# One weight split and one head's loads issued earlier in a fused attention and recurrence layer

## The chip, the cores and the metric

The kernel runs on one core of one Trainium2 chip. The metric is device time in microseconds (us); lower is better. The engines named below are TensorE (PE, matrix products; PEld is its weight load), VectorE (DVE), ScalarE (ACT), GpSimd (POOL) and SyncE (SP), which issues most of the transfers. Each engine works through its own list of instructions in order; between engines an instruction waits for the events it depends on.

## The reference

One layer of a hybrid encoder on 1024 tokens of width 1024, all in float32. Cut to what matters:

```python
h = layer_norm(x, emb_ln_g, emb_ln_b)
q, k, v, z_a, u, z_b, g_a, g_b = split(h @ w_in)
attn = neighbourhood_attention(q, k, v, rpb)     # 8 heads of 64, a window of 8 x 16 on a 16 x 64 grid
y_a = attn * silu(z_a)
u = centred_depthwise_conv(u, conv_w, conv_b)
h2 = rg_lru(u, ..., forward) + rg_lru(u, ..., reverse)
y_b = h2 * silu(z_b)
m = sigmoid(g_a + b_merge[0]) * (y_a @ w_ba) + sigmoid(g_b + b_merge[1]) * (y_b @ w_bb)
out = layer_norm(ALPHA * h + m @ w_out, ln_g, ln_b)
```

## The kernel before

Every large product is made of three: both operands are split into a high part in the matmul's own format and the low rest, and the kernel adds high x high, high x low and low x high (`mm3`, line 127). A weight tile therefore needs two instructions before it can be used: a cast that makes the high part, and a subtraction (`lo_of`, lines 124 and 125) that makes the low part.

The stages follow one another: the first layer norm and the v and q projections; sixteen pairs of projection columns with seven products each (`product`, slots 0 to 111), with the recurrence woven in; a short `ending`; attention; the merge of the two branches with their gates; the output product with the last layer norm. All engines' lists are in the order in which the Python code issues instructions; only buffers and waits are filled in behind.

**Between the projections and attention.** At slot `HEAD_AT` = 109 memory comes free, and `load_k(0)` (line 862) brings the keys of head 0 (1 MB with both copies; queries and bias of head 0 are loaded three slots earlier). In slots 112 to 114 `ending` (line 958) runs the first product of the recurrence branch's projection, in two column halves on two banks; it loads their gate tiles (`g_load(1, 0, k)`, line 939, 256 KB each), which VectorE multiplies in `b_gate` (line 954). In its third step it loads the next weight tile, two further gate tiles and, through `load_head(1)` (line 868), what head 1 needs: queries `qs` (line 858, 512 KB), bias (line 859, 448 KB) and keys `ks` (line 864, 1024 KB). Meanwhile the last gate results of the projections are still being stored (`gb_d`, line 652). All these transfers are issued by SyncE. The first load of values, `load_v(0)` (line 1026), follows.

**Attention.** Work goes in units of one block of 128 queries. A unit of head h holds `biased` (VectorE adds the bias to a score, line 1046), `turned` (TensorE transposes probabilities, line 1058), `values` (line 1082), `exped` (ScalarE, line 1051) and `score` for head h+1 (TensorE, line 1036), and some matmuls of the recurrence branch's projection as filling. Scores go into two banks in turn. Head 1's first score comes in unit 0, right behind the first transposes of head 0.

**The merge.** Eight weight tiles of the attention branch (`wb`, tag with two buffers) are used one after another; tile j serves two slots, one for each half n of the columns, with twelve matmuls each. `b_split(0, j, A)` (line 835) casts the high part on ScalarE (line 840) and makes the low part on GpSimd. `merge(j, n)` (line 1237) applies the gate and adds the other branch on VectorE (lines 956 and 1239), then casts the high part of the result on ScalarE (line 1241); `merge_lo` makes its low part. The output weights `wo` are split in the same loop (line 1280 on ScalarE, then GpSimd). The first two slots are irregular: their last three matmuls (k = 3 of tile 0) are held back until attention's last head is done, so tile 0 is read for the last time at the end of slot 2:

```python
run(b_group(0, j, n, ya, o, range(3 if slot < 2 else 4)))
if 0 < slot < 3:
    run(b_group(0, 0, slot - 1, ya, sums_m[slot - 1], range(3, 4)))
    merge(0, slot - 1, sums_m[slot - 1])
if n == 0 and j > 0:
    b_split(0, j + 1, A)
```

Tile (0,2), the third, is split in slot 2 and used from slot 4 on.

Of the kernel before, what the change touches and what calls it, by code (L numbers as in the profile page):

```python
# [35 lines left out]
HEAD_AT = 109  # L36
# [31 lines left out]
def encoder_kernel(ctx, tc, x, gb1, gb, w_qk, w_v, w_s, w_ba, w_bb, w_gate, smalls, bias, w_out, out):  # L68
# [3 lines left out]
    def pool(name, side="left", **kw):  # L72
        return tc.alloc_tile_pool(name=name, bufs=1, side=side, reuse_waits="tile", **kw)
# [13 lines left out]
    def bank(name):  # L87
        if turns:
            return banks[0].tile([P, HALF], F32, tag=next(turns[0]), bufs=2, name=name)
        return banks[0].tile([P, HALF], F32, tag="bank", name=name)  # L90
# [23 lines left out]
    def pair(pl, shape, name, **kw):  # L114
        return [pl.tile(shape, F32R, name=f"{name}_{c}", **({**kw, "tag": kw["tag"] + c} if "tag" in kw else kw))
                for c in "hl"]
# [7 lines left out]
    def lo_of(eng, lo, full, hi):  # L124
        eng.tensor_tensor(lo, full, hi.bitcast(F32), ALU.subtract)  # L125
# [10 lines left out]
    def run(gen):  # L136
        for _ in gen:
            pass
# [538 lines left out]
    def at(slot, pos, f):  # L677
        todo.setdefault((slot, pos), []).append(f)
# [151 lines left out]
    def b_load(which, j):  # L830
        if j < NK:
            st = b_w[which, j] = ev.tile([P, 4, P], F32, tag="z", bufs=5, name=f"wb{which}{j}")
            SP.dma_start(st[:], (w_ba, w_bb)[which][j])

    def b_split(which, j, eng=None):
        if j < NK:
            st = b_w[which, j]
            hi, lo = b_w[which, j] = pair(late["wb"], [P, 4, P], f"wb{which}{j}", tag="wb", bufs=2)
            if eng is A:
                A.copy(hi[:], st[:])  # L840
            else:
                G.tensor_copy(hi[:], st[:])  # L842
            lo_of(G, lo[:], st[:], hi[:])
# [10 lines left out]
    def load_q(h):  # L854
        hd = late["hd" if h % 2 else "hd0"]
        q = hd.tile([P, S], F32R, tag="qs", name=f"qs{h}")
        bt = hd.tile([P, BIAS_W], F32, tag="bias", name=f"bias{h}")
        SP.dma_start(q[:].bitcast(F32), q_d[h // 2][HALVES[h % 2][0]].rearrange("p z s -> (p z) s"))
        SP.dma_start(bt[:], bias[h])
        heads[h] = q, bt  # L860

    def load_k(h):
        k = late["hd"].tile([P, 2, S], F32R, tag="ks", bufs=2, name=f"ks{h}")
        SP.dma_start(k[:].rearrange("p z s -> p (z s)").bitcast(F32),
                     k_d[h // 2][HALVES[h % 2][0]].rearrange("p z s -> p (z s)").unsqueeze(1).to_broadcast([DH, 2, 2 * S]))
        heads[h] = heads[h][0], k, heads[h][1]

    def load_head(h):
        if h < H:
            load_q(h)  # L870
            load_k(h)
# [21 lines left out]
        at(slot + 3, 0, lambda t=t: yb_lo(t))  # L893
    at(HEAD_AT, 1, head_pool)
    at(HEAD_AT, 1, lambda: load_k(0))
    at(HEAD_AT - 3, 1, head_start)

    RHS = dict(a11=B11, s2=T2, s3=T3, s1=T1, a12=B21, a22=T4, s4=B22)
# [40 lines left out]
    def g_load(which, j, n, **kw):  # L939
        if j < NK:  # L940
            g = mt[which, j, n] = ev.tile([P, HALF], F32, name=f"g{which}{j}{n}", **(kw or dict(tag="z", bufs=5)))
            SP.dma_start(g[:], (ga_d, gb_d)[which][j][:, n * HALF:(n + 1) * HALF])

    def b_group(which, j, n, y, o, ks=range(4)):

        yield from mm3(o[:], [([t[:, k, :] for t in b_w[which, j]], [t[:, k, halves[n]] for t in y]) for k in ks],
                       quantum=1, first=ks[0] == 0, last=ks[-1] == 3)

    def b_gate(which, j, n, o):
        sl = slice(n * HALF, (n + 1) * HALF)  # L950
        g = mt.pop((which, j, n))
        if which == 1:
            m1 = late["m", j, n] = late["mp"].tile([P, HALF], F32, tag=f"m{j}{n}", name=f"m1{j}{n}")
            V.scalar_tensor_tensor(m1[:], g[:], 1.0, o[:], ALU.add, ALU.mult)
        else:
            V.scalar_tensor_tensor(o[:], g[:], 1.0, o[:], ALU.add, ALU.mult)

    def ending(k):

        if k == 0:  # L960
            for pl in (hts.pop(), hts.pop(), wsp, hb):
                pl.release()
            late["mp"] = pool("mp")
        if k == 2:
            b_load(1, 2)
            for n in range(2):
                g_load(1, 1, n)
            load_head(1)
        if k < 2:
            g_load(1, 0, k)  # L970
            late["o", k] = bank(f"mb10{k}")
            run(b_group(1, 0, k, late["yb"], late["o", k]))
        if 0 < k < 3:
            b_gate(1, 0, k - 1, late["o", k - 1])
# [3 lines left out]
    for slot in range(7 * N_PAIR + 4):  # L978
        p, k = divmod(slot, 7)
        if k == 0 and p < N_PAIR:  # L980
            takers[p], ub[p] = takes[p](), {}
        done = (p, k - 1) if k else (p - 1, 6)
        prep = (p + 1, OPS[k - 1]) if k else (p if p else N_PAIR, OPS[6])
        rest = evacuate(*done) if slot <= 7 * N_PAIR else []
        s_hi(*prep)
        for f in todo.pop((slot, 0), ()):
            f()
        for f in squashes:
            f()
        squashes = rest[:1]  # L990
        stores[slot + 2] = rest[1:]
        if p < N_PAIR:
            product(p, k)
        for o in lows:
            s_lo(*o)
        lows = [prep]
        for f in stores.pop(slot, ()):
            f()
        if k < 4:
            s_sum(p + 1, ("s1", "s2", "s3", "s4")[k])  # L1000
        elif k == 4:
            s_load(p + 2, "a11", "a21", "a12", "a22")
        for f in todo.pop((slot, 1), ()):
            f()
        if p == N_PAIR:
            ending(k)
# [156 lines left out]
    for unit in range(-NT, H * NT + PV_LAG):  # L1163
# [50 lines left out]
        if unit == H * NT:  # L1214
# [7 lines left out]
            def w_load(k):  # L1222
                if k < NK:
                    wos[k] = wop.tile([P, D], F32, tag="wos", bufs=3, name=f"wos{k}")
                    SP.dma_start(wos[k][:], w_out[k * P:(k + 1) * P, :])
# [9 lines left out]
    sums_m, mh, ml = {}, {}, {}  # L1235

    def merge(j, n, o):
        b_gate(0, j, n, o)
        V.tensor_tensor(o[:], o[:], late["m", j, n][:], ALU.add)
        mh[j, n] = late["mp"].tile([P, HALF], F32R, tag=f"m{j}{n}", name=f"mh{j}{n}")  # L1240
        A.copy(mh[j, n][:], o[:])

    def merge_lo(j, n, o):
        lo_of(V, ml[j, n][:], o[:], mh[j, n][:])
# [8 lines left out]
    for slot in range(2 * NK + 2):  # L1253
        j, n = divmod(slot, 2)
        if 2 < slot <= 2 * NK:
            merge(*divmod(slot - 1, 2), sums_m[slot - 1])
        if slot == 2:
            at0.release()
            mlp = pool("mlp")
            ml.update({(j, n): mlp.tile([P, HALF], F32R, name=f"ml{j}{n}") for j in range(NK) for n in range(2)})  # L1260
            wo += [pair(mlp, [P, D], f"wo{k}") for k in range(NK - 2, NK)]
            merge_lo(0, 0, sums_m.pop(0))
        for q in (1,) if slot == 3 else (slot - 2,) if slot > 3 else ():
            merge_lo(*divmod(q, 2), sums_m.pop(q))
        if j < NK:
            if n == 0:
                b_load(0, j + 2)
            g_load(0, j + 1, n, **(dict(tag=f"u{slot % 4}", bufs=1) if slot % 4 else dict(tag="z", bufs=5)))
            o = sums_m[slot] = bank(f"mb{j}{n}")

            run(b_group(0, j, n, ya, o, range(3 if slot < 2 else 4)))
            if 0 < slot < 3:
                run(b_group(0, 0, slot - 1, ya, sums_m[slot - 1], range(3, 4)))
                merge(0, slot - 1, sums_m[slot - 1])
            if n == 0 and j > 0:
                b_split(0, j + 1, A)

        if slot % 2:
            if j < NK:
                A.copy(wo[j][0][:], wos[j][:])  # L1280
            if j > 0:
                w_load(j + 2)
        elif slot > 0:
            lo_of(G, wo[j - 1][1][:], wos.pop(j - 1)[:], wo[j - 1][0][:])
        if slot == 9:
            zp = pool("zp")
            gb2 = zp.tile([P, 2, D], F32, name="gb2")
            zs = {}

            def load_z(i):  # L1290
                if i < NT:
                    zs[i] = zp.tile([P, D], F32, tag="z", bufs=4, name=f"z{i}")
                    SP.dma_start(zs[i][:], h_d[i])

        elif slot in (10, 12, 14):
            load_z(slot // 2 - 5)
        elif slot in (11, 13):
            SP.dma_start(gb2[:, :, halves[slot // 13]], gb[slot // 13])
# [146 lines left out]
```

## Time and profile before

| | |
|---|---|
| time, median of 3 runs | 683.49 us (683.47 to 684.93) |
| time of the profiled execution | 684.63 us |
| its span, first to last instruction | 682.8 us |
| its mean granted TensorE clock | 0.997 |
| matmul instructions | 3177 |
| moved by transfers | 113.40 MB, mean 166 GB/s |

A row of the profile's timeline has the start in us from the span's start, the length, the engine, the line of the kernel, the operation, output<-input and the number of instructions; in brackets stands the idle time before it and what ended that. SPq is SyncE's queue of issues: such a row is the issue of a transfer, not its duration. A row of waits has the waiting instruction, what it waited for, the total in us, how often, and the longest.

### The profile page before, as it was taken

What the parts mean: (1) busy time and instruction counts of PE and PEld (TensorE: products, weight loads), DVE (VectorE), ACT (ScalarE), POOL (GpSimd) and SP (SyncE); (2) the same over time, 40 slices, a digit from 0 to 9 for tenths busy, and PEclk for the clock granted to TensorE, in tenths of its full rate; (3) what the DMA queues carried; (4) which work ended last, traced back from release to release, by engine and by line L of the source; (5) the groups of instructions that cost most, each with busy time, mean ns of one, the idle gap of its engine ahead of it and who ended that gap; (6) DMA issues with size and microseconds to landing.
All of it is one profiled execution on the core that took longest, in us unless ns stands there. A gap on an engine that the chain in (4) does not pass through costs nothing.

```text
span 682.8 us, 9299 instructions
## 1 busy us (share of the span) xinstructions
PE 665.8 (98%) x3177; PEld 554.4 (81%) x3177; DVE 494.7 (72%) x821; ACT 363.9 (53%) x612; POOL 353.8 (52%) x258
## 2 busy tenths in 40 slices
PE   7999999999999999999999999999999999999995
PEld 6787888888888888888788888788888878888884
DVE  7866766796899599879977785378787777533434
ACT  4544524247686677768576634467777554310110
POOL 5697461444576577567647544115355446435442
PEclk9999999999999999999999999999999999999998
DMA  8654165223324233431453557898794457512211
GB/s 327 227 187 154 63 231 171 78 92 124 124 92 145 71 108 123 170 124 48 170 199 112 182 176 253 305 353 308 250 327 144 176 197 271 189 62 93 92 62 61
DMA packets 48703, 113.40 MB, mean 166 GB/s; under 512 B 5057, under 2 KB 9745, under 8 KB 47121
## 3 DMA queue, kind: packets, MB, share of 16 engines
q1 hardware_dynamic: 48624, 112.81, 47.4%
q8 instruction: 25, 0.41, 0.2%
q14 instruction: 22, 0.17, 0.1%
q10 hardware_dynamic: 32, 0.01, 0.0%
HBM read 77.11 MB, written 35.68 MB: 165 GB/s over the span
## 4 chain that ended last, share of the span: by engine, by line
PE 80%; DVE 8%; DMA 4%; POOL 3%; issue 2%; ACT 1%; SPq 1%; DVEq 0%; POOLq 0%; ACTq 0%
PE a L131 29%; PE o L131 13%; PE s L131 11%; PE mb L131 10%; PE q L131 5%; PE acc L1082 3%; PE pt L1058 3%; PE s L1036 3%; POOL x L243 2%; PE v L308 2%; PE g L734 2%; DMA wvsl<-in_w_v_dram 1%; DMA ks<-k_d 1%; DMA wb<-in_w_ba_dram 1%; DVE ws_l L125 1%
## 5 line engine op out<-in xcount | busy, mean ns | idle before, releaser
L131 PE MATMUL o<-wo_h,ml 128*128 128x512 f32 (+1 forms) x136 | 51.2, 377 | 0.0
L131 PE MATMUL o<-wo_l,mh 128*128 128x512 f32 (+1 forms) x136 | 51.2, 376 | 0.0
L131 PE MATMUL o<-wo_h,mh 128*128 128x512 f32 (+1 forms) x136 | 51.2, 376 | 0.0
L1046 DVE CUSTOM_DVE_ANT_0 sc<-s,bias 128x384 f32<-128x384 f32 (+1 forms) x64 | 33.5, 523 | 22.9 <-PE s L1036 14.0
L131 PE MATMUL a<-ht_h,ws_h 128*128 128x512 f32 x128 | 49.9, 390 | 0.0
L131 PE MATMUL a<-ht_h,ws_l 128*128 128x512 f32 x128 | 49.8, 389 | 0.0
L131 PE MATMUL a<-ht_l,ws_h 128*128 128x512 f32 x128 | 49.8, 389 | 0.0
L131 PE MATMUL a<-b_h,wa_h 128*128 128x512 f32 x128 | 49.8, 389 | 0.0
L131 PE MATMUL a<-b_h,wa_l 128*128 128x512 f32 x128 | 49.8, 389 | 0.0
L131 PE MATMUL a<-b_l,wa_h 128*128 128x512 f32 x128 | 49.8, 389 | 0.0
L1335 DVE SCALAR_TENSOR_TENSOR z<-z,o 128x512 f32<-128x512 f32 (+1 forms) x17 | 11.2, 656 | 51.0 <-PE o L131 51.0
L1066 ACT CAST pt_h<-pt 128x384 fp32r<-128x384 f32 x64 | 29.0, 453 | 26.4 <-PE pt L1058 18.3
L1345 POOL TENSOR_TENSOR z<-z,gb 128x1024 f32<-128x1024 f32 x7 | 16.8, 2395 | 48.5 <-ACT z L1344 48.5
L1051 ACT ACTIVATE p<-sc,summ 128x384 f32<-128x384 f32 (+1 forms) x64 | 37.9, 592 | 5.2 <-DVE summ L1046 5.0
L1314 ACT ACTIVATE sd<-mv,eps_z 128x1 f32<-128x1 f32 x8 | 2.4, 294 | 67.1 <-DVE mv L1340 67.1
L308 PE MATMUL v<-wv,b_h 128*128 128x512 f32 x128 | 32.8, 399 | 2.7 <-ACT b_h L263 1.6
L125 DVE TENSOR_TENSOR pt_l<-pt,pt_h 128x384 fp32r<-128x384 f32 x64 | 33.2, 519 | 2.1 <-ACT pt_h L1066 1.6
L1036 PE MATMUL s<-ks,qs 128*128 128x384 f32 (+1 forms) x128 | 31.3, 326 | 1.1 <-DMA ks<-k_d 1.1
L308 PEld LDWEIGHTS v<-wv,b_h 128*128 128x128 f32 x128 | 23.6, 188 | 9.3 <-ACT b_h L263 2.3
L842 POOL CAST wb_h<-wb 128x512 fp32r<-128x512 f32 x9 | 7.0, 777 | 46.1 <-PE s L1036 18.3
L125 POOL TENSOR_TENSOR wb_l<-wb,wb_h 128x512 fp32r<-128x512 f32 x16 | 22.0, 1374 | 16.1 <-ACT wb_h L840 15.4
L1058 PEld LDWEIGHTS pt<-ident,p 128*128 128x128 f32 x176 | 23.1, 140 | 8.5
(438 smaller groups left out, 2199.8 us busy)
## 6 DMA issues: line engine op xcount, KB each, us to landing
ks<-k_d SPq DMA_DIRECT2D x8, 1024.0 KB, 8.0
h_d<-x SPq DMA_DIRECT2D x8, 512.0 KB, 4.4
v_d<-vs SPq DMA_DIRECT2D x8, 512.0 KB, 3.7
q_d<-q SPq DMA_DIRECT2D x8, 512.0 KB, 3.0
ga_d<-ga SPq DMA_DIRECT2D x16, 256.0 KB, 2.0
gb_d<-gb SPq DMA_DIRECT2D x16, 256.0 KB, 2.0
k_d<-k SPq DMA_DIRECT2D x8, 512.0 KB, 4.0
qs<-q_d SPq DMA_DIRECT2D x8, 512.0 KB, 3.9
```

The source lines that it names most:

```text
L125: eng.tensor_tensor(lo, full, hi.bitcast(F32), ALU.subtract)
L131: PE.matmul(o, a, b, start=first and i == 0, stop=last and i == len(prods) - 1, skip_group_check=not (first and last))
L243: G.tensor_tensor(z[:, halves[c]], z[:, halves[c]], gb_t[w][c][:], op)
L308: PE.matmul(vos[i][:], a, wv[kind == "w"][k][:], start=vn[i] == 0, stop=vn[i] == 23)
L734: PE.matmul(o[:, n, :], w[:, 2 * d + b, :], us[b][:, n * HALF:(n + 1) * HALF], start=z == 0, stop=z == 1)
L1036: PE.matmul(o[:, :P * len(near(t))], q[:, t * P:(t + 1) * P], k[:, z, keys], start=z == 0, stop=z == 1)
L1046: V.tensor_tensor_reduce(s[:, :w], o[:, :w], heads[h][2][:, b0:b0 + w], -1.0, 3.0e38, ALU.add, ALU.min, accum_out=sums[h][0][:, t:t + 1])
L1051: A.activation(probs[h % 2][t][:], scs.pop((h, t))[:, :w], AF.Exp, bias=sums[h][0][:, t:t + 1], scale=-1.0, accum_out=sums[h][1][:, t:t + 1])
L1058: PE.transpose(tp[:, n * P:(n + 1) * P], probs[h % 2][t][:, z * P:(z + 1) * P], ident[:])
L1066: A.copy(pt[0][:, span(b)], tps[h, b][:, :P * len(near(b))])
L1082: PE.matmul(acc[g][:, d:d + w], vvs[h // 2][:, b, h % 2, :], pt[:, a:a + w], start=b in (1, 6) and z == 0, stop=z == 1 and b == (4, 7)[g])
L1345: G.tensor_tensor(z[:], z[:], gb2[:, 0, :], ALU.mult)
```

## The change

Two edits. `load_head(1)` moves from the third step of `ending` to slot `HEAD_AT`, right behind `load_k(0)`. And in the merge loop `b_split` stands between the held-back matmuls and their `merge`; among the slots to which both apply (1 and 2) only slot 2 has n = 0 and j > 0, so it is the split of tile (0,2) that moves, ahead of `merge(0, 1)`. All other instructions stay, in number and order.

```diff
     at(HEAD_AT, 1, head_pool)
     at(HEAD_AT, 1, lambda: load_k(0))
+    at(HEAD_AT, 1, lambda: load_head(1))
     at(HEAD_AT - 3, 1, head_start)
...
             b_load(1, 2)
             for n in range(2):
                 g_load(1, 1, n)
-            load_head(1)
         if k < 2:
...
             if 0 < slot < 3:
                 run(b_group(0, 0, slot - 1, ya, sums_m[slot - 1], range(3, 4)))
-                merge(0, slot - 1, sums_m[slot - 1])
             if n == 0 and j > 0:
                 b_split(0, j + 1, A)
+            if 0 < slot < 3:
+                merge(0, slot - 1, sums_m[slot - 1])
```

## The prediction, made before the changed kernel ran

> **What bounds the kernel now.** I read the busy shares first, then TensorE's waits, then the chain that ended last, and last the instructions around the two places that the change touches. The page's first part:
>
> ```profile
> PE 665.8 (98%) x3177; PEld 554.4 (81%) x3177; DVE 494.7 (72%) x821; ACT 363.9 (53%) x612; POOL 353.8 (52%) x258
> ```
>
> TensorE is busy for 98% of the span. Only its idle time, or another order of its work, can be won, and this change leaves TensorE's order alone. The view of waits for TensorE has these rows from 443 us to the end, and no others there:
>
> ```profile
> PE s L1036 <- DMA ks<-k_d: 1.1, 1, 1.1
> PE mb L131 <- POOL wb_l L125: 0.9, 1, 0.9
> PE mb L131 <- ACT wb_h L840: 0.5, 1, 0.5
> ```
>
> One wait is for the keys of a head; the other two are one stall, for the two halves of a weight tile. The chain that ended last runs through both:
>
> ```profile
> 434.73 8.79 DMA ks<-k_d
> ...
> 542.23 6.96 DMA wb<-in_w_ba_dram
> ...
> 553.49 1.29 POOL wb_l L125
> 554.82 32.71 PE mb L131 x143
> 587.53 87.36 PE o L131 x408
> ```
>
> Columns: start, length, what. After 554.82 TensorE works without a gap until the last products, so a microsecond taken out before it should reach the end.
>
> **First part: the second head's loads.** The keys `ks1` are issued at 434.73 and land at 443.52. TensorE around that moment:
>
> ```profile
> 442.10 0.49 PE L1058 MATMUL pt<-ident,p 128*128 128x128 f32 x3
> 443.65 0.47 PE L1036 MATMUL s<-ks,qs 128*128 128x256 f32 x2 [1.07 <-DMA ks<-k_d]
> ...
> 445.68 0.49 PE L1058 MATMUL pt<-ident,p 128*128 128x128 f32 x3
> 445.93 0.59 PE L1036 MATMUL s<-ks,qs 128*128 128x384 f32 x2
> ```
>
> Unhindered, a score starts 0.25 us after its three transposes (445.68 to 445.93). The stalled one started 1.55 us after, so the stall cost 1.30 us, a little over the 1.07 shown as idle. The three loads (queries, bias, keys) now stand right behind the first head's keys in SyncE's queue:
>
> ```profile
> 422.37 0.55 SPq L864 DMA_DIRECT2D ks<-k_d  x1
> 426.66 0.32 SPq L652 DMA_DIRECT2D gb_d<-gb  x1
> 427.07 0.38 SPq L942 DMA_DIRECT2D g<-gb_d  x1
> 429.72 0.38 SPq L942 DMA_DIRECT2D g<-gb_d  x1
> ...
> 433.79 0.42 SPq L858 DMA_DIRECT2D qs<-q_d  x1
> ...
> 436.70 0.54 SPq L1029 DMA_DIRECT2D vv<-v_d  x1
> ```
>
> The queue rests from 422.92 until the gate store at 426.66; three issues of some 0.5 us fit into that pause, so `ks1` is issued by about 424.5. What did 1 MB of keys take?
>
> ```profile
> DMA to landing us min/median/max: 4.7/8.0/9.2
> ```
>
> Even the longest, 9.2, lands at 433.7, against a need at 442.35. So the 1.30 us go, and head 0's own keys, 4.7 us alone, are wanted only for the first score, which VectorE reads at 436.58 (row below).
>
> What is late next? The loads are 512, 448 and 1024 KB; from 427 on they share the engines with two gate stores and the two gate loads of `ending` (256 KB each): 3,008 KB, 3.08 MB, up to the second gate load. VectorE needs those two loads here:
>
> ```profile
> 433.26 0.69 DVE L954 SCALAR_TENSOR_TENSOR m<-g,mb 128x512 f32<-128x512 f32 x1 [4.75 <-PE mb L131]
> 435.98 0.69 DVE L954 SCALAR_TENSOR_TENSOR m<-g,mb 128x512 f32<-128x512 f32 x1 [2.03 <-PE mb L131]
> 436.58 0.42 DVE L1046 CUSTOM_DVE_ANT_0 sc<-s,bias 128x256 f32<-128x256 f32 x1
> ```
>
> Queued behind the second `L954` on VectorE is the first biased score, and TensorE has two score banks, so it can run only two scores ahead of VectorE. A gate load later than 435.98 costs TensorE at most that lateness. How fast does the queue empty? Two rows of the view by stretches (the last two figures: share of the DMA engines, GB/s):
>
> ```profile
> 434.00:436.00 2.00, 2.00 (x11) 1.69 (x10) 0.02 (x1) 0.00 (x0) 0.00 (x0) 1.00 0.88 223
> 436.70:443.60 6.90, 5.88 (x31) 4.96 (x29) 4.64 (x17) 5.61 (x17) 1.30 (x1) 1.00 1.02 409
> ```
>
> The second stretch carries the same kinds of load and is full; at 409 GB/s 3.08 MB take 7.5 us. `ks0` landed at 422.37 + 4.7 = 427.07, so the second gate load would be in by 434.6: 1.4 us to spare. At the slowest, 223 GB/s, it would be 13.8 us and 440.9, a loss of 4.9. The first row is two microseconds in which the loads were only being issued, so I take the full stretch, and nothing for this cost; 0 to 4.9 stays for the range. The first `L954` may slip by 2 us without harm, since the gap of 2.03 us in front of the second hides it.
>
> The Trainium skill ("DMA: Bandwidth & Descriptors", section "Queues, rings and completion order") speaks against the move: each DMA engine takes descriptors in ring order, so a load issued behind 2 MB stands behind all of it. The same page puts the memory side at about 358 GB/s, which would make it 8.6 us and 435.7; the 409 in the row is above that. By the page the sum would be the same, with 0.3 us to spare.
>
> SyncE waits in order as well. In the changed kernel's instruction list the second (1,1) gate load waits for the first `L954` (over at 433.95) and, since eight completion counters are used in turn, for `ks1`; the first values load `vv` stands behind it. That puts `vv` at about 434.4 at the latest, against 436.70 before, while its reader comes only 1.3 us earlier. No cost.
>
> **Second part: the weight split.** In the changed list on ScalarE, the cast `wb_h` of tile (0,2) moves up past one cast, `mh` of (0,1); the cast of (1,0) already stood behind it. Nothing is added. ScalarE, GpSimd and TensorE there:
>
> ```profile
> 550.11 1.05 ACT L1280 CAST wo_h<-wos 128x1024 fp32r<-128x1024 f32 x1
> 552.31 0.58 ACT L1241 CAST mh<-mb 128x512 fp32r<-128x512 f32 x1 [1.15 <-DVE mb L1239]
> 552.79 0.62 ACT L840 CAST wb_h<-wb 128x512 fp32r<-128x512 f32 x1
> ...
> 555.56 0.59 ACT L1241 CAST mh<-mb 128x512 fp32r<-128x512 f32 x1 [0.39 <-DVE mb L1239]
> 556.04 0.62 ACT L840 CAST wb_h<-wb 128x512 fp32r<-128x512 f32 x1
> ```
> ```profile
> 553.49 1.28 POOL L125 TENSOR_TENSOR wb_l<-wb,wb_h 128x512 fp32r<-128x512 f32 x1 [7.76 <-ACT wb_h L840]
> 554.72 2.40 POOL L125 TENSOR_TENSOR wo_l<-wos,wo_h 128x1024 fp32r<-128x1024 f32 x1
> 557.08 1.30 POOL L125 TENSOR_TENSOR wb_l<-wb,wb_h 128x512 fp32r<-128x512 f32 x1
> ```
> ```profile
> 549.86 0.39 PE L131 MATMUL mb<-ya_l,wb_h 128*128 128x512 f32 x1
> ...
> 552.58 0.39 PE L131 MATMUL mb<-ya_l,wb_h 128*128 128x512 f32 x1
> 553.46 0.50 PE L131 MATMUL mb<-ya_h,wb_h 128*128 128x512 f32 x1 [0.50 <-ACT wb_h L840]
> 554.82 0.50 PE L131 MATMUL mb<-ya_h,wb_l 128*128 128x512 f32 x1 [0.86 <-POOL wb_l L125]
> 555.16 0.40 PE L131 MATMUL mb<-ya_l,wb_h 128*128 128x512 f32 x1
> ```
>
> The split can start when three things are there: its data (the chain's load, 542.23 + 6.96 = 549.19), its buffer (the last matmul that reads tile (0,0), 549.86 + 0.39 = 550.25) and ScalarE (`wo_h`, 550.11 + 1.05 = 551.16). The last decides: `wb_h` runs from 551.16 to 551.78, 1.6 us earlier. GpSimd, idle by then, follows 0.08 behind as before (553.41 to 553.49), 551.86 to 553.15. TensorE's twelve matmuls from 549.86 to 552.58 are 0.227 apart, so tile (0,2) is first wanted at 552.81, its low half at 553.03 and its high half again at 553.26. With the low half at 553.15 the second matmul starts near 553.2, and the third 0.23 to 0.34 later (0.34 is the spacing behind the old stall), at 553.43 to 553.54. It was at 555.16: a gain of 1.6 to 1.7; I take 1.7. The passed cast waits for VectorE until 552.3 anyway and loses nothing. If the load landed after 551.16 instead, the gain would shrink one for one.
>
> Late next would be tile (0,3). Its `wb_h` stays at 556.04, tied to VectorE through the cast at 555.56, but `wo_l` no longer stands in GpSimd's way (553.15 to 555.55), so `wb_l` runs from 556.74 to 558.04. TensorE wants it 24 matmuls (5.44 us) after 553.2, at 558.64. 0.6 us of slack; not a stall.
>
> **Sum.** 1.3 + 1.7 = 3.0 us. The profiled execution had a span of 682.8 and a time of 684.6 (1.8 outside the span), and would come to 681.6. The three runs shown are 683.47 to 684.93 with the profiled one near the top; from their median, 683.5 - 3.0 = 680.5.
>
> **Rivals.**
>
> *Only the split pays.* The profiled execution is 1.1 us above the median, about the size of the keys' stall. If that stall is small in most runs, or a late gate load gives the 1.3 back, 1.7 remains: 681.8. For it: landings vary widely for one size (4.7 to 9.2). Against it: the chain ties the issue of `ks1` to a store and a blocked queue, which any run has.
>
> *The split only moves the stall.* If tile (0,3) or VectorE's order of merges turns out to be what TensorE then waits for, little of the 1.7 stays: 683.5 - 1.3 = 682.2. Against it is the slack of 0.6, for it that this was computed with GpSimd at its usual 1.3 us.
>
> *Gate loads behind the 2 MB (slower).* Place: the second `L954`. Price: one for one from 435.98. It cancels both gains when the load takes over 9.3 us from its issue at 429.72, and shows as slower from 10.6 us. The gate loads of the whole run:
>
> ```profile
> DMA to landing us min/median/max: 2.5/4.9/8.5
> ```
>
> The median gives 434.6, the maximum 438.2 and a loss of 2.2, still a net gain. Only at the 223 GB/s would it land at 440.9: 683.5 - 3.0 + 4.9 = 685.4.
>
> **How the numbers follow.** Both gains: 0.67 (680.5). Only the split, or a partial loss at the gate loads: 0.17 (681.8). The stall moved: 0.11 (682.2). Slower: 0.05 (685.4). The range 679.6 to 682.4 holds the first three, with 0.9 below the forecast for two stalls that are larger in other runs than in the profiled one. 0.2% is 1.4 us, about what a measurement of this kernel tells from no change, so faster means below 682.1: the first case, nearly all of the second and a little of the third, 0.84; same 0.11; slower 0.05.
>
> **What would show it.** Right: no wait of TensorE for `ks` and the scores of head 1 straight behind the transposes; `ks1` landed before 434; `wb_h` ahead of the `mh` cast near 551 on this clock (some 549.9 with the first gain) and under 0.3 us of wait for `wb_l`. Wrong: a wait of `L954` for a gate load near 436 with TensorE stalled at the third score, a `wb` wait one tile later, or a new wait in the heads between, where the profile of before shows none.

## The result, and the profile after

| | before | changed |
|---|---|---|
| median of the runs | 683.48 us (683.09 to 684.93, 6 runs) | 681.35 us (681.14 to 681.54, 6 runs) |
| profiled execution: time, span | 684.63, 682.8 us | 681.54, 679.8 us |
| granted TensorE clock | 0.997 | 0.997 |

The ratio is 0.9963, with a 95% interval of 0.9950 to 0.9976: the kernel became faster, by 1.6 to 3.4 us. The medians alone differ by 2.1; here and below the ratio is not the quotient of the medians, so the two can differ by some tenths of a us. In the two profiled executions the difference is 3.0 in the span.

The view of waits for TensorE, from 400 us to the end of the changed kernel, has one row left in place of three:

```profile
PE mb L131 <- DVE ya_l L125: 0.2, 1, 0.2
```

The keys and both halves of the weight tile are gone from it. TensorE's timeline of the changed kernel at head 1's first score, with the first matmul of `ending` ahead of it (start, length, engine, line, operation):

```profile
429.89 0.39 PE L131 MATMUL mb<-yb_h,wb_h 128*128 128x512 f32 x1
...
441.65 0.49 PE L1058 MATMUL pt<-ident,p 128*128 128x128 f32 x3
441.89 0.48 PE L1036 MATMUL s<-ks,qs 128*128 128x256 f32 x2
```

The score now starts 0.24 us after its transposes, not 1.55. SyncE's queue in the changed kernel, and the first two gate products on VectorE:

```profile
421.92 0.55 SPq L864 DMA_DIRECT2D ks<-k_d  x1
422.53 0.59 SPq L858 DMA_DIRECT2D qs<-q_d  x1
423.16 0.42 SPq L859 DMA_DIRECT2D bias<-in_bias_dram  x1
423.63 0.54 SPq L864 DMA_DIRECT2D ks<-k_d  x1
...
426.63 0.39 SPq L943 DMA_DIRECT2D g<-gb_d  x1
...
429.23 0.48 SPq L943 DMA_DIRECT2D g<-gb_d  x1
...
435.78 0.42 SPq L1029 DMA_DIRECT2D vv<-v_d  x1
```
```profile
434.33 0.69 DVE L955 SCALAR_TENSOR_TENSOR m<-g,mb 128x512 f32<-128x512 f32 x1 [6.26 <-DMA g<-gb_d]
435.64 0.69 DVE L955 SCALAR_TENSOR_TENSOR m<-g,mb 128x512 f32<-128x512 f32 x1 [0.62 <-DMA g<-gb_d]
```

The three loads fit into the queue's pause, and head 1's keys landed 9.1 us after their issue, at 432.7, well before they are needed. But both gate products now wait for their transfer, where before they waited for TensorE. The view by stretches says how fast the queue emptied meanwhile (the last figures: TensorE's clock, DMA share, GB/s):

```profile
426.00:428.00 2.00, 2.00 (x10) 1.65 (x9) 0.63 (x1) 0.19 (x1) 0.00 (x0) 1.00 0.97 385
428.00:430.00 2.00, 2.00 (x11) 1.65 (x10) 0.07 (x1) 0.69 (x1) 0.00 (x0) 1.00 1.05 341
430.00:432.00 2.00, 2.00 (x11) 1.65 (x10) 0.00 (x0) 1.84 (x2) 0.00 (x0) 1.00 1.00 295
432.00:434.00 2.00, 2.00 (x11) 1.65 (x10) 0.00 (x0) 0.13 (x1) 0.00 (x0) 1.00 0.97 337
434.00:436.00 2.00, 2.00 (x11) 1.71 (x10) 1.05 (x2) 0.00 (x0) 0.00 (x0) 1.00 1.05 404
```

Full engines (a share of about 1.0), and yet 352 GB/s on average over these 10 us, with less than 345 in the three middle rows, not 409. Then the merge in the changed kernel, ScalarE, GpSimd and TensorE:

```profile
548.76 1.06 ACT L1281 CAST wo_h<-wos 128x1024 fp32r<-128x1024 f32 x1
549.72 0.62 ACT L840 CAST wb_h<-wb 128x512 fp32r<-128x512 f32 x1
550.96 0.59 ACT L1241 CAST mh<-mb 128x512 fp32r<-128x512 f32 x1 [0.63 <-DVE mb L1239]
```
```profile
550.41 1.30 POOL L125 TENSOR_TENSOR wb_l<-wb,wb_h 128x512 fp32r<-128x512 f32 x1 [6.04 <-ACT wb_h L840]
551.67 2.40 POOL L125 TENSOR_TENSOR wo_l<-wos,wo_h 128x1024 fp32r<-128x1024 f32 x1
555.40 1.29 POOL L125 TENSOR_TENSOR wb_l<-wb,wb_h 128x512 fp32r<-128x512 f32 x1 [1.33 <-ACT wb_h L840]
```
```profile
545.32 0.40 PE L131 MATMUL mb<-ya_h,wb_h 128*128 128x512 f32 x1
...
551.46 0.39 PE L131 MATMUL mb<-ya_h,wb_h 128*128 128x512 f32 x1
551.76 0.50 PE L131 MATMUL mb<-ya_h,wb_l 128*128 128x512 f32 x1
552.10 0.40 PE L131 MATMUL mb<-ya_l,wb_h 128*128 128x512 f32 x1
```

The split follows `wo_h` at once, GpSimd follows the split, and TensorE's second matmul of tile (0,2) comes 0.30 us after the first instead of 1.36. 545.32 is the 22nd matmul of the merge, the first of slot 2; 552.10 is the 51st. In the kernel before these two stand at

```profile
430.34 0.39 PE L131 MATMUL mb<-yb_h,wb_h 128*128 128x512 f32 x1
...
546.66 0.40 PE L131 MATMUL mb<-ya_h,wb_h 128*128 128x512 f32 x1
```

and at 555.16 (with the first matmul of `ending` at 430.34). So the time can be cut into stages that begin and end on TensorE. For each profile, in us:

| profile | start to `ending` | to head 1's first score | to the merge | to matmul 22 | to matmul 51 | to the end |
|---|---|---|---|---|---|---|
| before | 430.34 | 13.31 | 98.09 | 4.92 | 8.50 | 127.6 |
| changed | 429.89 | 12.00 | 98.15 | 5.28 | 6.78 | 127.7 |

The span fell by 3.0: 1.31 at the keys, 1.72 at the split and 0.45 before `ending`, where the kernels are alike; 0.36 was lost ahead of matmul 22, mostly the wait of the one row above (for the last head's result, behind two small transfers). In all profiles of this document that column has 4.89 to 5.08 where head 1's loads are in their old place (four profiles) and 4.85 to 5.66 where they are moved (nine). The ranges overlap and I do not count it to the change; but the three longest are all with the loads moved, and whether these have a part in it is not shown.

### The profile page after: what moved, and what is told of

It reads as the page before. It is cut to its first block, busy times and chain, and to the rows that moved or that the text cites. A ratio compares the mean times of both kernels' runs of the same rounds, so it can differ in the third digit from the quotient of the medians.

```text
span 679.8 us, 9295 instructions
## 1 busy us (share of the span) xinstructions
PE 665.4 (98%) x3177; PEld 554.7 (82%) x3177; DVE 493.8 (73%) x821; ACT 363.9 (54%) x612; POOL 354.3 (52%) x258
## 4 chain that ended last, share of the span: by engine, by line
PE 83%; DVE 8%; POOL 3%; DMA 3%; issue 1%; ACT 1%; SPq 0%; DVEq 0%; POOLq 0%; ACTq 0%
PE a L131 29%; PE o L131 13%; PE mb L131 12%; PE s L131 11%; PE q L131 5%; PE acc L1082 3%; PE s L1036 3%; PE pt L1058 3%; POOL x L243 2%; PE v L308 2%; PE g L734 2%; DMA wvsl<-in_w_v_dram 1%; DVE ws_l L125 1%; DVE uc L692 1%; DVE wa_l L125 1%
## 5 line engine op out<-in xcount | busy, mean ns | idle before, releaser
L1058 PE MATMUL pt<-ident,p 128*128 128x128 f32 x176 | 29.6, 272 | 0.0
```

The lines of the kernel that those rows point to most:

```text
L1058: PE.transpose(tp[:, n * P:(n + 1) * P], probs[h % 2][t][:, z * P:(z + 1) * P], ident[:])
```

## The experiments

All later comparisons have the kernel before beside them on the same chip.

**Each edit alone, and the gate loads first.** The first two kernels are the two hunks of the diff, one each; the third is the kernel before again for a second profile. The fourth is the changed kernel with

```diff
     at(HEAD_AT, 1, lambda: load_k(0))
+    for n in range(2):
+        at(HEAD_AT, 1, lambda n=n: g_load(1, 0, n))
     at(HEAD_AT, 1, lambda: load_head(1))
...
         if k < 2:
-            g_load(1, 0, k)
```

> Only the loads of head 1 are moved; the weight split stays where it was. Theory A (the stalls of the profile of before are the same in every execution): the wait of 1.1 us for the keys goes and the two waits for the weight tile stay, 0.5 and 0.9 us; time 1.3 us under before, about 682.2. Theory B (the keys' stall is what makes the runs of before fall into two groups, near 683.4 and near 684.9): the two groups become one, and the median falls by less than 1.3, to 682.8 or so, with a spread under 0.5.

> Only the split of tile (0,2) is moved up; head 1's loads stay where they were. Theory A: the wait for the keys stays at about 1.1 us, the wait for the weight tile goes, and the time falls by 1.5 to 1.7, to about 681.9. Theory B: the same fall, but the runs still fall into two groups about 1.5 us apart, near 681.9 and 683.4.

> The kernel before once more, for a second profile of it. Theory A: the keys' stall is 1.0 to 1.2 us of idle time again, whatever the time of this run. Theory B: where the run is near 683.4 the keys' stall is under 0.4 us, where it is near 684.9 it is 1.1 or more.

> The changed kernel with the two gate loads of the recurrence branch's first tile issued ahead of head 1's loads instead of behind them. If the gate loads stand behind the 2 MB in the changed kernel (the row of VectorE's wait of 6.3 us for a gate load says so), VectorE no longer waits for a gate load here and starts the first of them when its product is done, about 1.5 us earlier. Theory A (TensorE lost nothing to it, the lateness was hidden): the same time as the changed kernel, 681.3, within 0.2. Rival (a part of the missing 0.9 us was lost there): 0.3 to 0.9 faster, 680.5 to 681.0.

Here the kernel before took 684.45 us (median of 23 runs, 683.04 to 685.10, spread evenly and not in two groups, so the theories B of the first two kernels have nothing to explain). The loads alone: 683.81, ratio 0.9993 (0.9984 to 1.0001); this is less than the 1.3 us of theory A, and the time alone does not tell it from no change. The split alone: 682.86, 0.9983 (0.9974 to 0.9991). Before again: one run, 684.75. Gate loads first: 681.35, 0.9964 (0.9952 to 0.9976), the same ratio as the changed kernel's 0.9963, so nothing beyond it.

TensorE's waits in the profiles of the loads alone, of the split alone, and of the kernel before again:

```profile
PE mb L131 <- POOL wb_l L125: 0.9, 1, 0.9
PE mb L131 <- ACT wb_h L840: 0.5, 1, 0.5
```
```profile
PE s L1036 <- DMA ks<-k_d: 0.9, 1, 0.9
```
```profile
PE mb L131 <- POOL wb_l L125: 0.9, 1, 0.9
PE s L1036 <- DMA ks<-k_d: 0.7, 1, 0.7
PE mb L131 <- ACT wb_h L840: 0.5, 1, 0.5
```

Each edit removes its own wait and leaves the other's. The weight tile's two waits are the same every time; the keys' wait is not (1.1, 0.7, 0.9). Both theories on the second profile of the kernel before fail: the wait is under the 1.0 to 1.2 us of theory A, and theory B wanted 1.1 or more in a run as slow as 684.75.

**How close the gate loads are.** The first kernel is the changed one with one more line behind head 1's loads, a copy of 1 MB within the device memory that nothing reads; the second has the same copy and the gate loads first:

```diff
     at(HEAD_AT, 1, lambda: load_head(1))
+    at(HEAD_AT, 1, lambda: SP.dma_start(ex_d[:], w_out[0:2 * P, :].rearrange("(p a) d -> p (a d)", a=2)))
```

> The changed kernel with one more transfer in the queue, right behind head 1's keys: a copy of 1 MB from one place of the device memory to another, which nothing reads. Theory A (transfers are served about in the order of issue at some 335 GB/s, and a gate load later than TensorE's second product of that stage costs TensorE one for one): 3.1 us more in front of the gate loads, the second L955 on VectorE near 438.7 instead of 435.6, TensorE waits some 2.9 us around the third score, time 684.3. Rival (a load issued later does not stand behind it, or the lateness is hidden): under 0.5 us, 681.9 or less.

> The same extra copy of 1 MB, but with the two gate loads issued ahead of head 1's loads. Theory A: the gate loads are in time again (first L957 not waiting for a transfer), and the keys of head 1 and the first values have slack enough, so the loss of the run with the copy alone goes away: about 681.5. Rival (the loss comes from another transfer than the gate loads, such as the keys or the values): the loss stays, 683 or more.

The kernel before took 684.62 in this comparison (15 runs). With the copy: 684.58, 1.0008 (0.9997 to 1.0019), so that the whole gain is gone. In its profile 2.27 us of that are lost up to head 1's first score (14.27 against 12.00 in the table of stages below). The theory had 2.9 from a second gate product near 438.7; it came at 438.06. With the copy and the gate loads first: 681.74, 0.9968 (0.9956 to 0.9981), and it is back (up to head 1's first score as short as ever, 12.01; the next stage, 98.38, is 0.2 longer). VectorE with the copy, then TensorE there, then VectorE with the gate loads first (lines are 1 to 4 higher than in the changed kernel):

```profile
436.72 0.69 DVE L957 SCALAR_TENSOR_TENSOR m<-g,mb 128x512 f32<-128x512 f32 x1 [8.52 <-PE s L1038]
438.06 0.69 DVE L957 SCALAR_TENSOR_TENSOR m<-g,mb 128x512 f32<-128x512 f32 x1 [0.66 <-DMA g<-gb_d]
438.67 0.41 DVE L1048 CUSTOM_DVE_ANT_0 sc<-s,bias 128x256 f32<-128x256 f32 x1
```
```profile
439.15 0.62 PE L1038 MATMUL s<-ks,qs 128*128 128x384 f32 x2 [2.00 <-DVE summ L1048]
```
```profile
432.44 0.69 DVE L959 SCALAR_TENSOR_TENSOR m<-g,mb 128x512 f32<-128x512 f32 x1 [4.74 <-PE mb L132]
435.16 0.69 DVE L959 SCALAR_TENSOR_TENSOR m<-g,mb 128x512 f32<-128x512 f32 x1 [2.03 <-PE mb L132]
```

The chain is to be read from top to bottom: the second gate product starts late, the first biased score stands behind it, and TensorE's third score waits for that score's bank. The release named for the first `L957` is the last event by the profile, but TensorE's product was long done there; SyncE's order and the run with the gate loads first say that it is the transfer. That the loss goes away when two loads of 256 KB are put first, with the same bytes in flight, shows that the gate loads cause it, and not the keys or the values.

**One more cast out of the way.** The changed kernel with the cast `wo_h` of the first output weights moved from slot 1 to slot 2, behind the split of tile (0,2):

```diff
         if slot % 2:
-            if j < NK:
+            if 0 < j < NK:
                 A.copy(wo[j][0][:], wos[j][:])
...
                 b_split(0, j + 1, A)
+            if slot == 2:
+                A.copy(wo[0][0][:], wos[0][:])
```

> The changed kernel with the split of tile (0,2) moved up by one more cast on ScalarE, ahead of the cast of the first output weights wo. It then starts when the buffer comes free (the last matmul that reads tile (0,0)) and not when ScalarE comes free, 0.9 us earlier, and the low half is ready before TensorE wants it. Theory A: the rest of 0.2 us that the profile after shows between the first and the third matmul of tile (0,2) goes, 6.78 us there become 6.58; in the time 0.2, within its noise. Rival (the cast of wo then delays the next cast mh or the low half of tile (0,3)): a new wait of TensorE in slot 6.

Matmul 22 to 51 took 6.63 us, and no wait is left on TensorE after 400 us. The time was 681.45, 0.9961 (0.9948 to 0.9975), beside 681.63 for the changed kernel. It is the lowest of this comparison, but 0.15 us cannot be told from noise in the time; only the stage shows it.

**The changed kernel again, and the edits alone again.**

> The changed kernel once more, with more rounds. By the stages of the profiles so far (keys' stall 0.95 to 1.31 us, split 1.72 us, start of the program 0.9 us up or down from one execution to the next) it should be 2.7 to 3.0 under before: about 681.5 where before is 684.4. If the first comparison's 2.1 is the true size, it is 682.3.

> Head 1's loads alone once more, beside the other two on one chip, because the medians of the two edits alone (0.6 and 1.6 under before) add up to 2.2 and the changed kernel was 3.0 under. Theory A (the edits add up, as the stages of the profiles say; the rest is the start of the program): 1.0 to 1.3 under before. Rival (alone, this edit is worth less in most executions than in the profiled ones): 0.6 or less again.

> The split alone once more. Theory A: 1.7 under before. Rival (the two edits help each other): 1.2 to 1.4 under before, less than the 1.7 of the stage.

> The changed kernel beside them. Theory A: 2.7 to 3.0 under before and equal to the sum of the two others within 0.4. Rival: 0.6 or more beyond that sum.

The changed kernel beside the copies: 681.63 against 684.62, ratio 0.9966 (0.9953 to 0.9978). On a further chip, where the kernel before took 684.16 (23 runs): loads alone 683.62, 0.9992 (0.9981 to 1.0002); split alone 682.66, 0.9979 (0.9967 to 0.9990); both 681.10, 0.9962 (0.9948 to 0.9975). The stages of these profiles:

| profile | start to `ending` | to head 1's first score | to the merge | to matmul 22 | to matmul 51 | to the end |
|---|---|---|---|---|---|---|
| before again | 430.62 | 12.95 | 98.15 | 5.08 | 8.50 | 127.7 |
| loads alone | 430.18 | 12.00 | 98.17 | 5.07 | 8.50 | 127.7 |
| loads alone, second | 430.59 | 11.98 | 98.15 | 4.85 | 8.49 | 127.6 |
| split alone | 430.39 | 13.11 | 98.12 | 4.92 | 6.78 | 127.7 |
| split alone, second | 429.27 | 12.56 | 98.14 | 4.89 | 6.77 | 127.7 |
| changed, second | 429.14 | 12.23 | 98.13 | 5.38 | 6.78 | 127.6 |
| changed, third | 429.69 | 12.06 | 98.19 | 4.90 | 6.78 | 127.7 |
| gate loads first | 430.89 | 12.00 | 98.15 | 5.07 | 6.77 | 127.6 |
| extra copy | 430.03 | 14.27 | 98.16 | 5.66 | 6.78 | 127.9 |
| extra copy, gate loads first | 429.52 | 12.01 | 98.38 | 5.10 | 6.78 | 127.8 |
| split ahead of `wo` | 430.35 | 12.04 | 98.09 | 5.09 | 6.63 | 127.6 |

The column that ends at matmul 51 is steady: 8.49 to 8.50 without the moved split, 6.77 to 6.78 with it. The column that ends at head 1's first score is not: 0.56 to 1.31 us over the 12.0 where the keys come late. In the second profile of the split alone, the keys were issued at 433.85 and landed 7.8 us later, at 441.7. The stall of 0.56 names no transfer, but without it the score would have started at 441.27, before that landing:

```profile
441.02 0.49 PE L1058 MATMUL pt<-ident,p 128*128 128x128 f32 x3
441.83 0.47 PE L1036 MATMUL s<-ks,qs 128*128 128x256 f32 x2 [0.32 <-DVE summ L1046]
```

What is open: in both comparisons the medians of the two edits alone add up to less than both together (0.6 and 1.6 against about 3.0; 0.5 and 1.5 against 3.1). By these medians the rivals came out for the loads alone (0.6 or less) and for both edits together (0.6 or more beyond the sum), and not the theories A; the split alone, 1.5, lies between its theory and its rival. The ratios give 0.5 and 1.2 against 2.3, and 0.5 and 1.4 against 2.6, each uncertain by 0.6 to 0.9 us either way. The stages show no place where one edit would help the other: the places that the edits touch gain 1.0 us (a mean) and 1.72. The start of the program, where no kernel differs, moves by 1.8 us between profiles (429.14 to 430.89), and it happens to be short in the three profiles of the changed kernel (429.6 on average, against 430.5 in the two of the kernel before). The runs do not decide between chance and a cause there. So the gain of the loads is shown by the stage, not by the time.

## Why the prediction held, point by point

**The split: mechanism and size.** 1.7 was forecast, and the profiles with and without the moved split differ by 1.71 to 1.73. The details hold too: ScalarE's `wo_h` decided the start of the split, not the load or the buffer (with that cast out of the way the stage became 6.63); a small rest was left, TensorE's second matmul 0.30 after the first; the passed cast `mh` lost nothing, since it still waited for VectorE; and tile (0,3) did not become the next stall. Its low half was there at 555.40 + 1.29 = 556.69, and TensorE wanted it 24 matmuls after 551.76, at 557.2: 0.5 us of slack, where 0.6 was worked out. The rival in which the stall only moves falls.

**The keys: mechanism right, size too constant.** The stall goes entirely, as forecast. The term was 1.30 us, from one profile; four profiles without the edit have 1.31, 0.95, 1.11 and 0.56, a mean of 1.0. The rival that only the split pays had asked whether the stall is small in most executions: it is smaller in three of the four, though not gone.

**The queue behind them: the term that was mis-sized.** The prediction let 3.08 MB flow at 409 GB/s and found 1.4 us to spare at the second gate product. The mechanism was right, the rate was not: between the landing of head 0's keys (421.92 + 4.8 = 426.7) and the second gate product (435.64) the engines, again full, moved 350 GB/s, and nothing was left to spare. The product started 435.64 - 429.89 = 5.75 us after the first matmul of `ending`, against 435.98 - 430.34 = 5.64 before. The rate of one full stretch did not carry over to another. The prediction also kept a loss of 0 to 4.9 for the range, but its range ends at 682.4, and a loss of more than 1.9 would have been outside it. The first gate load was about 1.5 us late and was hidden by the pause in front of the second, as forecast.

By the Trainium skill ("DMA: Bandwidth & Descriptors", section "Queues, rings and completion order") each DMA engine takes descriptors in ring order. The trace agrees: the second gate load, issued at 429.23 behind the 2 MB, was in only at about 435.6. An estimate with the 358 GB/s of the same page (section "Specifications") has the load in 0.3 us before the need, nearer to the trace than the 1.4 from the row.

The price of a late gate load was forecast as one for one. It is: 0.11 us late in the changed kernel and 0.0 lost; 0.19 late in its third profile and 0.06 lost; 0.39 late in its second (435.17 against 429.14 + 5.64) and 0.23 lost; 2.39 late with the extra copy and 2.27 lost. Some 0.11 to 0.16 are free, the rest is paid in full. The slower rival was thus a real mechanism that the change just misses. That it missed it is in part luck, since the 1.4 us of room on which the forecast of no cost rested were not there; one more megabyte was enough to bring the time to 684.58.

**The values load.** It was forecast to be issued at 434.4 at the latest, and was issued at 435.78. The wait that the prediction named, of the second (1,1) gate load for the first gate product, was over at 435.02, before SyncE came to that load at 435.35. What held SyncE were two waits ahead of it, for stores of gate results that now stood behind the 2 MB as well (rows of SyncE's waits in the changed kernel, from 420 to 440 us):

```profile
SPq L833 <- DMA gb_d<-gb: 2.2, 1, 2.2
SPq L943 <- DMA gb_d<-gb: 1.1, 1, 1.1
```

The issue is still earlier than the 436.70 before, and no wait of TensorE for the values appears; no cost.

**The time.** 680.5 was forecast and 681.35 measured, 0.85 more. The sum against the profiled execution was 681.6, and the profiled execution of the changed kernel took 681.54. That this agrees within 0.1 is luck in part: the program's start was 0.45 shorter there and the way to matmul 22 0.36 longer, which the sum did not have. The forecast subtracted 3.0 from the median of three runs, 683.49, and took the profiled 684.63 for a high one. In the first comparison, whose six runs of the kernel before include those three, the median is the same (683.48), and the changed kernel was only 2.1 under it. Larger samples of the kernel before, in the later comparisons, have medians of 684.45, 684.62 and 684.16; there the profiled one is ordinary, and the changed kernel is 3.0 and 3.1 under by the medians, 2.3 and 2.6 by the ratios. A base that was low by chance would explain much of the 0.85, and the keys' stall, 1.0 on average and not 1.3, some of it; how much belongs to each is not shown.

## What to carry to other kernels

Where an engine is busy all the time, a stall on it can be priced by the spacing of its own instructions on either side, as at the weight split, where the price came out the same within 0.02 us in every profile. Where a transfer decides, as at the keys, one profile is not enough: it had 1.31, and the mean of four was 1.0. A load that is moved ahead pushes back everything issued behind it, so the smallest and soonest needed transfers go first: here the two gate loads of 256 KB cost nothing in front of the 2 MB and are on the edge behind it. The base needs as much care as the sum that is subtracted from it: medians of three and six runs of the kernel before were 0.7 to 1.1 us below those of 15 to 23 runs, about a third of the sum.

## What the runs showed of the hardware

A wait of TensorE costs more than the idle time that the profile shows for it. At the weight tile 0.50 and 0.86 us of idle were 1.87 of time (8.50 with both waits, 6.63 with none); at the keys 1.07 was 1.30. The rows say where the rest is: a matmul row is 0.39 long, but the next one starts 0.227 after it, so idle time is counted from the end of a row and misses the first 0.16; and behind the wait a row is 0.50 long, and the next matmul starts 0.34 after it began.

The rate at which fully occupied DMA engines move data differs from stretch to stretch: 409 GB/s over 6.9 us of the kernel before, 295 to 404 in stretches of 2 us of the changed one, all with a share of about 1.0. What sets the rate was not tested.
